# The first three tiles of a phase multiplied before the norm is known, in a two-layer decoder trunk

## Chip, cores and metric

One core of a Trainium2 chip runs the whole kernel in one launch. The metric is the time of an execution on the device in microseconds (us). Time before: 1978.98 us, the median of 3 runs (1977.27 to 1979.56).

## What is computed

256 tokens of width 1024 pass two layers. Each has a mixer (layer 0: mLSTM and block attention; layer 1: differential attention) and a product-key expert network, PEER, with 8 heads, 128 keys per half and 128x128 experts. Ahead of each stands an RMSNorm with scale and shift that depend on a conditioning vector. Cut to what matters here:

```python
def rms_norm(x, g):
    y = xf * lax.rsqrt(jnp.mean(xf * xf, axis=-1, keepdims=True) + EPS)
    return y * g

h = rms_norm(x, norm_mix_g[layer]) * (1.0 + sc1) + sh1
x = x + g1 * mixer(h)                 # layer 0: mlstm_moba_mixer, layer 1: diff_attention_mixer
h = rms_norm(x, norm_ffn_g[layer]) * (1.0 + sc2) + sh2
x = x + g2 * peer_ffn(h, ...)

# peer_ffn: qry = h @ wq (16 slices of 128), sub = qry . keys,
# top 16 of 128 per half, top 16 of the 256 sums, then
# sum over the experts chosen of gate * gelu(u_e . h) * v_e
```

## The kernel before

**Layout and tiles.** Activations lie transposed, features on the partitions: `xT` is 8 blocks (`kd`) of 128 features by 256 tokens. A column tile of a weight matrix is 1024x128, one DMA of 512 KB on SP's queue into a ring of `raw` buffers (`load`, L146). Float32 products are made of three: ACT casts the weight to its high part `hi` (L159), DVE subtracts to get the low part `lo` (L162), both into rings of three in `stream`; the activation has `hhi` and `hlo` likewise. `mm_col` issues for every kd hi by hhi (L185), hi by hlo (L186), lo by hhi (L187): 24 matmuls of 128x256 a tile. The first three tiles of a phase run together, each two kd behind the one before it (`SKEW`), 72 matmuls, so that they can follow `h` as it is made; the tiles after them run one by one (`col_tiles`, L191).

**The program.** Four phases follow each other: mixer0 (to 184 us of the span), peer0 (to 1003), mixer1 (to 1157), peer1 (to the end). A phase starts where the phase before writes the last block of the residual `xT` (L414 after a mixer, L952 after the peer). Each block is squared on ACT (L279), added up on DVE (L281, but for the last block), and the sum over the features is taken by matmuls with a column of ones (L290). `keep_warm` (L268) puts 3 and 5 matmuls of zeros around these (`WARM`). Then DVE makes the mean (`nv`, L299, L301), POOL the power -1/2 (`nr`, L262), PE spreads it over the partitions (L306, result `rb`), and `norm_apply` makes per kd: `ht` = x times channel weight `gsc` times `rb` on DVE (L315), `hhi` = ht + shift on ACT (L318), `hlo` on DVE (L328). `first_tiles` (L208) and the list `late` place the splits of the first three weight tiles between these steps.

**A peer** (`peer_body`, L819) takes 16 tiles of `wq`: tile i gives a query copy `qry` on ACT (L849), a score matmul pair per tile (`scores`, L976), a copy `sub` (L979) and the top-16 search on DVE (L985 to L989: MAX, MAX_INDEX, MATCH_REPLACE, MAX, MAX_INDEX per half and head). A credit (`credit`, from -3.0, more for every tile) decides how many of these stand on DVE behind the `lo` of each tile. After the 16 tiles, 128 tiles of `u` follow (`h_tile`), their search work still spread in between, and then the products with `v` (L921 to L923).

**Mixer1** (`mixer1`, L707) takes 16 q and k tiles and two blocks of values (L237 to L239). Each q tile with its k tile makes a head (`diff_head`): squares (L360), their sums by matmul (L363), DVE (`qv`, L365), POOL's power (`qr`, L262), PE (L372), two copies to `qrows` (L374, L375) and PE again (L382). Between, DVE multiplies the modulation weights of the later phases (`ada`, L252), whose raw tiles come through the same ring. All engines run their instructions in order.

## Time and profile before

| what | value |
| --- | --- |
| median of 3 runs | 1978.98 us |
| profiled execution, its own time | 1980.2 us |
| its span | 1978.4 us |
| PE busy | 1932.3 us, 98% |
| DVE, ACT busy | 1481.9 us, 75%; 1123.5 us, 57% |
| POOL busy | 47.1 us, 2% |
| chain that ended last | 87% PE, 6% issue, 3% DVE |

The span is the stretch from the first to the last instruction that the profiler saw; the execution's time is a little longer. The chain follows, from the last instruction back, what each one waited for.

### The profile page before, as it was taken

Reading aid. Unit: us, or ns where it says so; the run is one execution under the profiler, and the core shown is the slowest. Engines: PE = TensorE matmul, PEld = TensorE weight load, DVE = VectorE, ACT = ScalarE, POOL = GpSimd, SP = SyncE. Lnnn points to the kernel's source line nnn. Section 1 sums busy time; section 2 is a strip of 40 time slices with the busy share of each in tenths; the row PEclk is TensorE's granted clock in tenths of the full one; section 3 lists DMA queues with packets and bytes.
Section 4 is the critical chain, followed back from the end, with each engine's and each line's share of the span. In section 5 each row is a group of like instructions: output and inputs, shape, how many; then the busy total and the mean of one; then the engine's idle time right before and its main releaser. Section 6 shows DMA issues by size and latency. Waiting matters only on the chain.

```text
span 1978.4 us, 34700 instructions
## 1 busy us (share of the span) xinstructions
PE 1932.3 (98%) x13229; PEld 1754.7 (89%) x13229; DVE 1481.9 (75%) x3064; ACT 1123.5 (57%) x2137; POOL 47.1 (2%) x37
## 2 busy tenths in 40 slices
PE   5999999999999999999999999999999999999999
PEld 4888999999999788888878799999999988888887
DVE  8987999678887566777568789987788865556655
ACT  4655555777775444444456555557777744444443
POOL 0020000000000000000012100000000000000000
PEclk7999999999999999999999999999999999999999
DMA  8863355445445677898347233554545455559660
GB/s 333 289 207 133 108 174 190 162 165 164 161 160 171 194 220 217 327 349 299 129 168 235 75 136 118 184 181 153 171 151 170 160 163 195 196 193 359 226 201 22
DMA packets 103990, 376.43 MB, mean 190 GB/s; under 512 B 11536, under 2 KB 12944, under 8 KB 103696
## 3 DMA queue, kind: packets, MB, share of 16 engines
q1 hardware_dynamic: 103824, 374.22, 56.0%
q8 instruction: 104, 1.70, 0.3%
q14 instruction: 62, 0.51, 0.1%
HBM read 373.12 MB, written 1.05 MB: 189 GB/s over the span
## 4 chain that ended last, share of the span: by engine, by line
PE 87%; issue 6%; DVE 3%; DMA 2%; ACT 1%; POOL 1%; POOLq 0%; ACTq 0%; DVEq 0%
PE ps_h L185 15%; PE ps_h L187 14%; PE ps_h L186 14%; PE ps_acc L921 11%; PE ps_acc L923 11%; PE ps_acc L922 11%; PE ps_g L1108 3%; DMA raw<-in_ada_w_dram 1%; PE ps_l L389 1%; DVE raw L252 1%; PE ps_acc L976 1%; DVE lo L162 1%; PE ps_h L237 1%; PE ps_h L239 1%; PE ps_h L238 1%
## 5 line engine op out<-in xcount | busy, mean ns | idle before, releaser
L159 ACT CAST hi<-raw 128x1024 fp32r<-128x1024 f32 x613 | 644.8, 1053 | 714.4 <-PE ps_acc L922 313.4
L162 DVE TENSOR_TENSOR lo<-raw,hi 128x1024 fp32r<-128x1024 f32 x613 | 748.2, 1221 | 347.0 <-ACT hi L159 344.6
L185 PE MATMUL ps_h<-h,hi 128*128 128x256 f32 x2504 | 725.6, 290 | 8.0 <-ACT h L449 3.4
L187 PE MATMUL ps_h<-h,lo 128*128 128x256 f32 x2504 | 712.3, 285 | 0.4 <-DVE lo L162 0.4
L186 PE MATMUL ps_h<-h,hi 128*128 128x256 f32 x2504 | 711.5, 284 | 0.4 <-DVE h L451 0.4
L185 PEld LDWEIGHTS ps_h<-h,hi 128*128 128x128 f32 x2504 | 481.9, 193 | 13.9 <-ACT h L449 4.2
L187 PEld LDWEIGHTS ps_h<-h,lo 128*128 128x128 f32 x2504 | 481.9, 192 | 2.8 <-DVE lo L162 1.1
L186 PEld LDWEIGHTS ps_h<-h,hi 128*128 128x128 f32 x2504 | 482.5, 193 | 1.9 <-DVE h L451 0.7
L921 PE MATMUL ps_acc<-hi,act 128*128 128x512 f32 x1024 | 399.2, 391 | 5.6 <-ACT act L902 5.6
L922 PE MATMUL ps_acc<-hi,act 128*128 128x512 f32 x1024 | 400.0, 391 | 0.0
L923 PE MATMUL ps_acc<-lo,act 128*128 128x512 f32 x1024 | 399.8, 391 | 0.0
L921 PEld LDWEIGHTS ps_acc<-hi,act 128*128 128x128 f32 x1024 | 192.6, 188 | 45.6 <-ACT act L902 6.0
L922 PEld LDWEIGHTS ps_acc<-hi,act 128*128 128x128 f32 x1024 | 193.2, 189 | 41.1 <-DVE act L903 0.7
L923 PEld LDWEIGHTS ps_acc<-lo,act 128*128 128x128 f32 x1024 | 192.8, 188 | 40.4 <-DVE lo L162 0.7
L252 DVE CUSTOM_DVE_ANT_0 raw<-raw,crow,small 128x1024 f32<-128x1024 f32 x96 | 122.7, 1279 | 23.0 <-DMA raw<-in_ada_w_dram 22.9
L1085 ACT ACTIVATE oi<-iota,it 128x128 f16<-128x128 f16 x320 | 108.0, 406 | 0.0
L1095 DVE TENSOR_TENSOR og<-oj,gt 128x1024 f16<-128x1024 f16 x128 | 87.8, 686 | 12.4 <-PE ps_g L1108 12.2
L1116 DVE TENSOR_TENSOR A<-A,ps_g 128x256 f32<-128x256 f32 (+25 forms) x214 | 69.2, 346 | 31.0 <-PE ps_g L1108 30.3
L969 ACT ACTIVATE A<-ps_h 128x256 f32<-128x256 f32 (+20 forms) x240 | 76.9, 321 | 3.9 <-PE ps_h L187 3.9
L903 DVE TENSOR_TENSOR act<-A,act 128x1024 fp32r<-128x1024 f32 x64 | 77.8, 1218 | 0.0
L1108 PE MATMUL ps_g<-oi,og 128*128 128x128 f16 x1024 | 73.3, 222 | 0.0
L902 ACT CAST act<-A 128x1024 fp32r<-128x1024 f32 x64 | 72.2, 1131 | 0.0
(305 smaller groups left out, 1671.6 us busy)
## 6 DMA issues: line engine op xcount, KB each, us to landing
raw<-in_uT_dram SPq DMA_DIRECT2D x256, 512.0 KB, 3.5
raw<-in_v_dram SPq DMA_DIRECT2D x256, 512.0 KB, 4.4
raw<-in_ada_w_dram SPq DMA_DIRECT2D x96, 512.0 KB, 5.2
raw<-in_wq_dram SPq DMA_DIRECT2D x32, 512.0 KB, 4.5
raw<-in_ev_in_dram SPq DMA_DIRECT2D x21, 512.0 KB, 5.0
raw<-in_od_in_dram SPq DMA_DIRECT2D x16, 512.0 KB, 4.6
raw<-in_ev_v_dram SPq DMA_DIRECT2D x8, 512.0 KB, 4.0
raw<-in_ev_out_dram SPq DMA_DIRECT2D x8, 512.0 KB, 4.4
```

What stands on the lines that cost most here:

```text
L159: nc.scalar.copy(hi, raw)
L162: self.last_lo = nc.vector.tensor_tensor(out=lo, in0=raw, in1=hi.bitcast(F32), op=ALU.subtract)
L185: nc.tensor.matmul(ps, lhsT=whi[:, s], rhs=ahi[:, kd, :], start=kd == kds[0], stop=False)
L186: nc.tensor.matmul(ps, lhsT=whi[:, s], rhs=alo[:, kd, :], start=False, stop=False)
L187: nc.tensor.matmul(ps, lhsT=wlo[:, s], rhs=ahi[:, kd, :], start=False, stop=kd == kds[-1])
L252: nc.vector.tensor_tensor_reduce(w, w, self.crow, 1.0, self.small[:, ab:ab + 1], ALU.mult, ALU.add, m)
L921: nc.tensor.matmul(acc[q], lhsT=xhi, rhs=vhi[:, c], start=m == 0, stop=False)
L922: nc.tensor.matmul(acc[q], lhsT=xlo, rhs=vhi[:, c], start=False, stop=False)
L923: nc.tensor.matmul(acc[q], lhsT=xhi, rhs=vlo[:, c], start=False, stop=m == NEXP - 1)
L1085: nc.scalar.activation(oi[:, k, :], self.iota, AF.Square, scale=-1.0, bias=tabs["i"][:, t0 + k:t0 + k + 1])
L1095: nc.vector.tensor_tensor(out=og, in0=oj.unsqueeze(1).to_broadcast(og.shape), in1=tabs["g"][:, :, ts].unsqueeze(2).to_broadcast(og.shape), ...
L1108: nc.tensor.matmul(pv[:, k, :], lhsT=og[:, w, :, k], rhs=oi[:, k, :], start=w == 0, stop=w == 1)
```

## The change

At the start of peer0, mixer1 and peer1 the first three tiles are no longer made from `h`. `raw_start` forms `pre` = x times `gsc`, not normalised, as a high part (8 ACTIVATE, L220) and a low part (8 on DVE, L221), with two more columns that hold the shift (L216, L217), and multiplies the three tiles with these: 72 matmuls of 128x258. Their weight splits lie in buffers of their own (`first`) and not in the ring of three. `raw_finish` turns the sums into outputs `fz`: the shift's column is copied (L230), the sum is multiplied by the norm factor on DVE (L231) and the shift's product added on ACT (L232). `norm_rstd` and `norm_apply` come behind, for the tiles 3 and on, of which three run together now in mixer1 and in the peers (`phase_tiles`). `WARM` is (0, 0): the 24 matmuls of zeros go, and the last square is added on DVE, so that one pair of sums (L308) is left of two. `first_tiles` and `late` go. The pools move: a peer's `wq` ring (5 buffers) lies in a pool of its own that closes before `A0` opens, and mixer1's ring has 9 buffers in place of 10. In mixer0 two pool names move, its instructions don't. The diff, cut to its core:

```diff
@@ -38,11 +38,9 @@
 V0_AT = 5
 SIDE_P2 = 52
 SKEW = 2
-LATE1 = ("stat", (None, 2), (None, 4))
-LATEP = (None, None, (None, 3))
 ROWS0 = {4: 1, 5: 1, 6: 1, 7: 1, 8: 4}
 AHEAD = 2
-WARM = (3, 5)
+WARM = (0, 0)
 SIDE_AT = 14
 LATE_RING = 15
...
@@ -207,21 +194,52 @@
             self.ready.append(self.wsplit(self.feed.pop(0)))
         return self.ready.pop(0)
 
...
+    @staticmethod
+    def next_raw(pool, bufs):
+        return pool.tile([P, 1024], F32, tag="raw", name="raw", bufs=bufs)
+
+    def raw_start(self, pool, layer, which, aps, tags, homes=()):
+
+
+        nc = self.nc
+        self.outs = [pool.tile([P, T], F32, tag="fz", name="fz", bufs=3) for _ in tags]
+        self.rstd = pool.tile([P, T], F32, name="rstd")
+        pre = pool.tile([P, 2, KD, T + 2], F32R, name="pre")
         ring, self.raw_ring = self.raw_ring, self.stream_ring
+        raws = [self.load(a) for a in aps[:len(tags)]]
         self.raw_ring = ring
+        pairs = list(homes)
+        pairs += [pool.tile([P, 2, 1024], F32R, tag=f"f{i}", name="first") for i in range(len(pairs), len(tags))]
+        ws = [self.split(raw, (p[:, 0], p[:, 1])) for raw, p in zip(raws, pairs)]
+        sh0 = 0 if which == 0 else 24
+        sh = self.mod[:, layer, sh0:sh0 + KD].unsqueeze(2).to_broadcast([P, KD, 2])
+        nc.scalar.copy(pre[:, 0, :, T:], sh)
+        nc.vector.tensor_tensor(out=pre[:, 1, :, T:], in0=sh, in1=pre[:, 0, :, T:].bitcast(F32), op=ALU.subtract)
+        for kd in range(KD):
+            x, g = self.xT[:, kd, :], self.gsc[:, layer, which, kd:kd + 1]
+            nc.scalar.activation(pre[:, 0, kd, :T], x, AF.Copy, scale=g)
+            nc.vector.scalar_tensor_tensor(pre[:, 1, kd, :T], x, g, pre[:, 0, kd, :T].bitcast(F32), op0=ALU.mult,
+                                           op1=ALU.subtract)
+        pss = [self.psum(t) for t in tags]
+        self.mm_col([ps[:, :T + 2] for ps in pss], ws, (pre[:, 0], pre[:, 1]))
+        return pss
+
+    def raw_finish(self, pool, ps, rstd, z):
+
+        b = pool.tile([P, 1], F32, tag="fb", name="fb", bufs=3)
+        self.nc.scalar.copy(b, ps[:, T:T + 1])
+        self.nc.vector.tensor_mul(z, ps[:, :T], rstd)
+        self.nc.scalar.activation(z, z, AF.Identity, bias=b)
+        return z
+
+    def phase_tiles(self, pool, aps, first, rb, act, tags, rest=None):
+
+        self.nc.scalar.copy(self.rstd, rb)
+        done = [self.raw_finish(pool, ps, self.rstd, z) for ps, z in zip(first, self.outs)]
+        n = len(first)
+        yield from enumerate(done)
+        for i, ps in self.col_tiles(aps[n:], act, tags, ws=[self.take(a) for a in aps[n:n + len(tags)]], rest=rest):
+            yield n + i, ps
 
     def mm_row(self, pss, aps, act):
 
...
@@ -707,22 +720,25 @@
     def mixer1(self):
         nc, tc, hp = self.nc, self.tc, self.hp
         w_in = self.io["od_in"]
-        ws = self.first_tiles([w_in[0], w_in[8], w_in[1]], LATE1)
         with ExitStack() as st:
             pool = st.enter_context(tc.tile_pool(name="mix1", bufs=1, reuse_waits="tile"))
             self.psum_phase(st, "psm1")
-            self.raw_ring = (pool, 10)
+            cols = [w_in[8 * k + hd] for hd in range(NH) for k in range(2)]
+            self.raw_ring = (pool, 9)
+            homes = [pool.tile([P, 2, 1024], F32R, tag=t, name="first") for t in ("yhi", "ylo")]
+            ht = pool.tile([P, KD, T], F32, tag="v", name="ht")
+            bias = self.alibi(pool)
+            first = self.raw_start(pool, 1, 0, cols, ("l", "l", "t"), homes)
             h = hp.tile([P, 2, KD, T], F32R, tag="x", name="h")
             hhi, hlo = h[:, 0], h[:, 1]
-            self.norm_apply(1, 0, self.norm_rstd(), pool.tile([P, KD, T], F32, tag="ylo", name="ht"), hhi, hlo)
+            rb = self.norm_rstd()
+            self.norm_apply(1, 0, rb, ht, hhi, hlo)
             h = (hhi, hlo)
-            with tc.issue_after(self.last_h.ins), tc.issue_after(self.last_t.ins):
-                self.qk_setup(pool, Cols.od_qn, Cols.od_kn)
-                og = pool.tile([P, 1], F32, name="og")
-                nc.vector.tensor_scalar_mul(og, self.small[:, Cols.onorm:Cols.onorm + 1], 1.0 - LAM_INIT)
-                bias = self.alibi(pool)
-            v = pool.tile([P, TT, 1024], F32, name="v")
-            yhi = pool.tile([P, KD, T], F32R, name="yhi")
+            self.qk_setup(pool, Cols.od_qn, Cols.od_kn)
+            og = pool.tile([P, 1], F32, name="og")
+            nc.vector.tensor_scalar_mul(og, self.small[:, Cols.onorm:Cols.onorm + 1], 1.0 - LAM_INIT)
+            v = pool.tile([P, TT, 1024], F32, tag="v", name="v")
+            yhi = pool.tile([P, KD, T], F32R, tag="yhi", name="yhi")
             ylo = pool.tile([P, KD, T], F32R, tag="ylo", name="ylo")
             lam = pool.tile([P, 1], F32, name="lam")
             live, zs, vhave = [], [], [0]
@@ -734,10 +750,9 @@
                     yield
                 vhave[0] = 4 * n + 4
 
-            cols = [w_in[8 * k + hd] for hd in range(NH) for k in range(2)]
             od_v = [[self.io["od_v"][n, w4] for w4 in range(4)] for n in range(2)]
             self.feed = cols[3:V0_AT + 1] + od_v[0] + cols[V0_AT + 1:V1_AT + 1] + od_v[1] + cols[V1_AT + 1:]
-            for i, ps in self.col_tiles(cols, h, ("h", "h", "l"), ws=ws):
+            for i, ps in self.phase_tiles(pool, cols, first, rb, h, ("t", "h", "h")):
                 z = pool.tile([P, T], F32, tag="z", name="z", bufs=8)
                 self.last_z = nc.scalar.copy(z, ps)
                 zs.append(z)
@@ -818,33 +833,35 @@
 
     def peer_body(self, layer, side, st):
         nc, tc = self.nc, self.tc
-        ws = self.first_tiles([self.io["wq"][layer, i] for i in range(3)], LATEP)
         self.psum_phase(st, f"psp{layer}")
         tab = st.enter_context(tc.tile_pool(name=f"tab{layer}", bufs=1, reuse_waits="tile"))
         oh = st.enter_context(tc.tile_pool(name=f"oh{layer}", bufs=2, reuse_waits="tile"))
         hp = self.hp
-        a0 = st.enter_context(tc.tile_pool(name=f"a0{layer}", bufs=1, reuse_waits="tile"))
+        wqp = tc.tile_pool(name=f"wqp{layer}", bufs=1, reuse_waits="tile")
+        wp = wqp.__enter__()
         tabs = {"i": tab.tile([P, T], F32, name="it"), "j": tab.tile([P, T], F16, name="jt"),
                 "g": tab.tile([P, 2, T], F16, name="gt")}
-        A0 = a0.tile([P, 32, T, 2], F32, name="A0")
-
-        scr = tc.tile_pool(name=f"scr{layer}", bufs=1, reuse_waits="tile")
+        scr = tc.tile_pool(name=f"scr{layer}", bufs=1, reuse_waits="tile", side="right")
         sp = scr.__enter__()
         h2 = hp.tile([P, 2, KD, T], F32R, tag="x", name="h2")
         hhi, hlo = h2[:, 0], h2[:, 1]
         ht = sp.tile([P, KD, T], F32, tag="eq", name="ht", bufs=1)
-        self.norm_apply(layer, 1, self.norm_rstd(), ht, hhi, hlo)
+        self.raw_ring = (wp, 5)
+        self.next_raw(*self.raw_ring)
+        wq = [self.io["wq"][layer, i] for i in range(16)]
+        first = self.raw_start(wp, layer, 1, wq, ("acc",) * 3)
+        rb = self.norm_rstd()
+        self.norm_apply(layer, 1, rb, ht, hhi, hlo)
         h = (hhi, hlo)
 
         keys = sp.tile([P, 2, P], F32, name="keys")
         nc.sync.dma_start(keys, self.io["keysT"][layer])
         vals = sp.tile([P, TT, 16, TOPK], F32, name="vals")
         idxs = sp.tile([P, TT, 16, TOPK], U32, name="idxs")
-        self.raw_ring = (sp, 5)
         subs = []
         topk = chain(self.stage1(sp, subs, vals, idxs), self.top_k(sp, vals, idxs, tabs))
         credit, live = -3.0, True
-        for i, ps in self.col_tiles([self.io["wq"][layer, i] for i in range(16)], h, ("acc",) * 3, ws=ws):
+        for i, ps in self.phase_tiles(wp, wq, first, rb, h, ("acc", "h", "h")):
             q = sp.tile([P, T], F32, tag="qry", name="qry", bufs=2)
             nc.scalar.copy(q, ps)
             if i:
@@ -858,8 +875,10 @@
                     credit -= next(topk)
 
         self.raw_ring = self.stream_ring
+        wqp.__exit__(None, None, None)
+        a0 = st.enter_context(tc.tile_pool(name=f"a0{layer}", bufs=1, reuse_waits="tile"))
         u, v = self.io["uT"][layer], self.io["v"][layer]
-        A, i = [A0], 0
+        A, i = [a0.tile([P, 32, T, 2], F32, name="A0")], 0
         while live:
             self.h_tile(u[i], h, A, i)
             if i == 0:
```

Where the instructions stand now. **ACT at the start of peer0.** `sq` are the squares, `first` the weight casts of the first three tiles, `hi` those of the tiles after. Before:

```order
L279 ACTIVATE sq<-xT 128x256
L159 CAST hi<-raw 128x1024
L279 ACTIVATE sq<-xT 128x256 x2
L159 CAST hi<-raw 128x1024
L318 ACTIVATE h_2066<-ht,mod 128x256 x8
```

And with the change:

```order
L297 ACTIVATE sq<-xT 128x256 x3
L154 CAST first<-raw 128x1024
L297 ACTIVATE sq<-xT 128x256
L154 CAST first<-raw 128x1024 x2
L216 CAST pre<-mod 128x8x2
L220 ACTIVATE pre<-xT,gsc 128x256 x8
L154 CAST hi<-raw 128x1024 x3
L230 COPY fb<-ps_acc 128x1 x3
L336 ACTIVATE h_2037<-ht,mod 128x256 x8
L237 COPY rstd<-ps_g 128x256
L154 CAST hi<-raw 128x1024
L232 ACTIVATE fz<-fz,fb 128x256 x3
```

All eight `pre` stand behind the square of the last block (the single L297) and behind two weight casts; the three `fz` stand behind the cast of tile 6.

**DVE in peer0 around the weight tiles 6 to 8** (`lo` the low part of a weight tile, MAX, MAX_INDEX and MATCH_REPLACE the search). Before, the `lo` of tiles 7 and 8 and what stands between them:

```order
L162 TENSOR_TENSOR lo<-raw,hi 128x1024
L988 MAX vals<-mr 128x8
L985 MAX vals<-sub 128x8
L989 MAX_INDEX idxs<-vals,mr 128x8
L986 MAX_INDEX idxs<-vals,sub 128x8
L987 MATCH_REPLACE mr<-vals,sub 128x128
L162 TENSOR_TENSOR lo<-raw,hi 128x1024
```

And with the change, where the search begins:

```order
L231 TENSOR_TENSOR fz<-ps_acc,rstd 128x256 x3
L155 TENSOR_TENSOR lo<-raw,hi 128x1024 x2
L1004 MAX vals<-sub 128x8 x2
L1005 MAX_INDEX idxs<-vals,sub 128x8
L1006 MATCH_REPLACE mr<-vals,sub 128x128
L1005 MAX_INDEX idxs<-vals,sub 128x8
```

The two `lo` are those of tiles 6 and 7. From the first MAX 43 search instructions follow in a row, and then the `lo` of tile 8. Before, the same 43 stood 18, 10, 10 and 5 ahead of the `lo` of the tiles 5, 6, 7 and 8. From that `lo` on both orders are the same.

**PE in mixer1 behind the second three tiles** (L363 is L377 now, L372 is L386, L382 is L396, L753 is L768, L237 is L255). Before:

```order
L186 MATMUL ps_h<-h,hi 128x256
L363 MATMUL ps_g<-ind_83,qsq 128x2 x2
L753 MATMUL ps_g<-lam_pr,ones 128x2
L187 MATMUL ps_h<-h,lo 128x256
L185 MATMUL ps_h<-h,hi 128x256
L363 MATMUL ps_g<-ind_83,qsq 128x2 x2
```

And with the change:

```order
L174 MATMUL ps_h<-h,lo 128x256
L377 MATMUL ps_g<-ind_83,qsq 128x2 x2
L768 MATMUL ps_g<-lam_pr,ones 128x2
L377 MATMUL ps_g<-ind_83,qsq 128x2 x2
L386 MATMUL ps_g<-ident,qr 4x128 x2
L377 MATMUL ps_g<-ind_83,qsq 128x2 x2
L396 MATMUL ps_g<-qrows,qsel 128x256 x2
L377 MATMUL ps_g<-ind_83,qsq 128x2 x2
L255 MATMUL ps_h<-hi,h 128x512
```

The head's small products stood among the matmuls of the tiles 3 to 5; now those tiles are done before them, and nothing of a tile stands between.

## Rows read from the trace of the kernel before

**Rows 1.** The page, part 1: busy time, share, instructions of each engine.

```profile
PE 1932.3 (98%) x13229; PEld 1754.7 (89%) x13229; DVE 1481.9 (75%) x3064; ACT 1123.5 (57%) x2137; POOL 47.1 (2%) x37
```

**Rows 2.** Windows: busy by engine; before the DMA share stands PE's granted clock.

```profile
184.00:189.00 5.00, 3.83 (x24) 2.40 (x22) 1.82 (x7) 1.77 (x4) 0.70 (x1) 1.00 0.80 238
204.00:224.00 20.00, 20.00 (x170) 19.88 (x169) 20.00 (x92) 9.55 (x18) 0.00 (x0) 1.00 0.43 145
224.00:274.00 50.00, 50.00 (x419) 49.75 (x418) 49.24 (x205) 23.60 (x39) 0.00 (x0) 1.00 0.35 117
1007.60:1014.00 6.40, 5.17 (x22) 4.88 (x23) 5.02 (x11) 2.32 (x5) 0.06 (x1) 0.50 0.01 3
```

**Rows 3.** Timeline, start of peer0: start, duration, engine, instruction, count, [idle before].

```profile
184.13 0.28 PE L187 MATMUL ps_h<-yhi,lo 128*128 128x256 f32 x1
184.44 0.48 DVE L414 SCALAR_TENSOR_TENSOR xT<-ps_h,mod,xT 128x256 f32<-128x256 f32 x1 [0.36 <-PE ps_h L187]
185.02 0.42 ACT L279 ACTIVATE sq<-xT 128x256 f32<-128x256 f32 x1 [2.21 <-DVE xT L414]
185.34 1.03 ACT L159 CAST hi<-raw 128x1024 fp32r<-128x1024 f32 x1
...
187.32 0.71 PE L306 MATMUL ps_g<-ident,nr 128*128 128x128 f32 x4
...
189.14 0.61 PE L185 MATMUL ps_acc<-h,hi 128*128 128x256 f32 x3 [1.11 <-ACT h L318]
...
189.78 0.39 PE L186 MATMUL ps_acc<-h,hi 128*128 128x256 f32 x1
```

**Rows 4.** Timeline of DVE, peer0: the last `hlo`, the search, the weight `lo`.

```profile
195.38 0.48 DVE L328 SCALAR_TENSOR_TENSOR h<-ht,mod,h 128x256 fp32r<-128x256 f32 x1 [0.19 <-ACT h L318]
...
200.31 0.48 DVE L985 MAX8 vals<-sub 128x8 f32<-128x128 f32 x2
...
211.48 1.21 DVE L162 TENSOR_TENSOR lo<-raw,hi 128x1024 fp32r<-128x1024 f32 x1
212.61 0.28 DVE L988 MAX8 vals<-mr 128x8 f32<-128x128 f32 x1
...
213.78 1.21 DVE L162 TENSOR_TENSOR lo<-raw,hi 128x1024 fp32r<-128x1024 f32 x1
...
220.73 1.20 DVE L162 TENSOR_TENSOR lo<-raw,hi 128x1024 fp32r<-128x1024 f32 x1
```

**Rows 5.** Timeline of PE, peer0: score matmuls, each ahead of a tile.

```profile
198.20 1.06 PE L976 MATMUL ps_acc<-keys,qry 128*128 128x128 f32 x8
199.01 0.36 PE L185 MATMUL ps_h<-h,hi 128*128 128x256 f32 x1
...
208.61 0.61 PE L976 MATMUL ps_acc<-keys,qry 128*128 128x128 f32 x4
...
222.11 0.61 PE L976 MATMUL ps_acc<-keys,qry 128*128 128x128 f32 x4
```

**Rows 6.** Timeline, mixer1: last block of x, first three tiles, what follows them.

```profile
1003.12 0.48 DVE L952 SCALAR_TENSOR_TENSOR xT<-ps_h,mod,xT 128x256 f32<-128x256 f32 x1
...
1010.86 0.41 PE L186 MATMUL ps_h<-h,hi 128*128 128x256 f32 x1
...
1021.06 1.28 DVE L252 CUSTOM_DVE_ANT_0 raw<-raw,crow,small 128x1024 f32<-128x1024 f32 x1
...
1023.08 2.61 POOL L262 TENSOR_TENSOR qr<-qv,mhalf 128x8 f32<-128x8 f32 x1 [4.38 <-DVE gsc L255]
...
1025.75 0.38 PE L372 MATMUL ps_g<-ident,qr 128*4 128x128 f32 x2 [0.46 <-POOL qr L262]
...
1026.56 0.41 DVE L375 TENSOR_TENSOR qrows<-ps_g,qrows 4x256 fp32r<-4x256 f32 x1
...
1033.97 0.48 PE L237 MATMUL ps_h<-hi,h 128*128 128x512 f32 x1
```

**Rows 7.** The page, part 6: count, KB each, median us from issue to landing.

```profile
raw<-in_ada_w_dram SPq DMA_DIRECT2D x96, 512.0 KB, 5.2
```

More of the change, by code (lines that the diff above doesn't have):

```diff
@@ L89, in setup @@
         self.raw_ring = self.stream_ring = (self.stream, 3)
-        self.feed, self.ready, self.late = [], [], []
+        self.feed, self.ready = [], []
         self.tmp = ctx.enter_context(tc.tile_pool(name="tmp", bufs=2, reuse_waits="tile"))
@@ L150, in load, with split @@
         return raw
-    def split(self, raw, late=None):
+    def split(self, raw, parts=None):
         nc = self.nc
-        hi = self.stream.tile([P, 1024], F32R, tag="hi", name="hi")
-        lo = self.stream.tile([P, 1024], F32R, tag="lo", name="lo")
-        def high():
-            nc.scalar.copy(hi, raw)
-        def low():
-            self.last_lo = nc.vector.tensor_tensor(out=lo, in0=raw, in1=hi.bitcast(F32), op=ALU.subtract)
-        for part, kd in zip((high, low), late or (None, None)):
-            if kd is None:
-                part()
-            else:
-                self.late.append((kd, part))
+        hi, lo = parts or [self.stream.tile([P, 1024], F32R, tag=t, name=t) for t in ("hi", "lo")]
+        nc.scalar.copy(hi, raw)
+        self.last_lo = nc.vector.tensor_tensor(out=lo, in0=raw, in1=hi.bitcast(F32), op=ALU.subtract)
         return hi, lo
@@ L208, in take @@
         return self.ready.pop(0)
-    def first_tiles(self, aps, late):
-        ring, self.raw_ring = self.raw_ring, self.stream_ring
-        ws = []
-        for a, when in zip(aps, late):
-            if when == "stat":
-                with self.tc.issue_after(self.last_sq.ins), self.tc.issue_after(self.last_add.ins):
-                    ws.append(self.split(self.load(a)))
-            elif when and when[0] is None:
-                with self.tc.issue_after(self.last_sq.ins):
-                    ws.append(self.split(self.load(a), when))
-            else:
-                ws.append(self.split(self.load(a), when))
-        self.raw_ring = ring
-        return ws
+    @staticmethod
@@ L314, in norm_apply @@
         for kd in kds:
-            self.last_t = nc.vector.scalar_tensor_tensor(t[:, kd, :], self.xT[:, kd, :], self.gsc[:, layer, which, kd:kd + 1], r,
-                                                         op0=ALU.mult, op1=ALU.mult)
+            nc.vector.scalar_tensor_tensor(t[:, kd, :], self.xT[:, kd, :], self.gsc[:, layer, which, kd:kd + 1], r,
+                                           op0=ALU.mult, op1=ALU.mult)
             sh = self.mod[:, layer, sh0 + kd:sh0 + kd + 1]
-            self.last_h = nc.scalar.activation(hhi[:, kd, :], t[:, kd, :], AF.Identity, bias=sh)
+            nc.scalar.activation(hhi[:, kd, :], t[:, kd, :], AF.Identity, bias=sh)
             if kd > kds[0]:
                 self.norm_lo(layer, sh0, t, hhi, hlo, kd - 1)
-            self.late.sort(key=lambda e: e[0])
-            while self.late and self.late[0][0] <= kd:
-                with self.tc.issue_after(self.last_h.ins), self.tc.issue_after(self.last_t.ins):
-                    self.late.pop(0)[1]()
         self.norm_lo(layer, sh0, t, hhi, hlo, kds[-1])
@@ L436, in mixer0 @@
             r = self.norm_rstd()
-            xn = pool.tile([P, KD, T], F32, tag="yhi", name="xn")
+            xn = pool.tile([P, KD, T], F32, tag="qk", name="xn")
             for half in range(2):
@@ L499, in mixer0 @@
                     bias = self.alibi(pool)
+                    yhi, ylo = [pool.tile([P, KD, T], F32R, name=n) for n in ("yhi", "ylo")]
                     self.qk_setup(pool, Cols.ev_qn, Cols.ev_kn)
@@ L875, in peer_body @@
         scr.__exit__(None, None, None)
-        a1p = tc.tile_pool(name=f"a1{layer}", bufs=1, reuse_waits="tile")
+        a1p = tc.tile_pool(name=f"a1{layer}", bufs=1, reuse_waits="tile", side="right")
         A.append(a1p.__enter__().tile([P, 32, T, 2], F32, name="A1"))
@@ L896, in peer_body @@
                     a1p.__exit__(None, None, None)
-                    late = st.enter_context(tc.tile_pool(name=f"late{layer}", bufs=1, reuse_waits="tile"))
+                    late = st.enter_context(tc.tile_pool(name=f"late{layer}", bufs=1, reuse_waits="tile", side="right"))
                     self.raw_ring = (late, LATE_RING)
```

4 lines of the change are left out of this document (1 added, 3 removed).

## Prediction

> **What bounds the kernel now.** I read the page's busy shares first, then the windows, then the timeline of each place that the change touches. PE is busy for 1932.3 of 1978.4 us [rows 1]: only 46 us of the span are not matmul, so a change at the phase starts can gain no more than the holes that stand there, and each new hole on PE is lost time, since nothing later has room to make it up. The windows show where the next engine stands behind PE [rows 2]: in peer0 from 204 to 224 us DVE is busy for 20.00 of 20.00 us, and from 224 to 274 for 49.24 of 50.00. PE is full there too. In this stretch of a peer, then, two engines are both at their limit, and whatever comes late on DVE stays late. Below 0.2% (4 us) a measurement of this kernel can't tell a change from none.
>
> **The hole that the change goes for.** The last matmul of mixer0 starts at 184.13 and PE could go on at 184.25; the first product of peer0 starts at 189.14, the first that needs h's low part at 189.78, and from there 72 products run at one per 0.12 us until 198.20 [rows 3, 5]. So 5.3 us of PE hold only sums, zeros and one small broadcast. The same picture stands ahead of peer1. In mixer1 the last x is written at 1003.12 and the steady products begin at 1010.86 [rows 6].
>
> **Peer: the first three tiles.** What they wait for now is `pre`, and by the order all of it stands on ACT behind the last square and two weight casts. From rows 3: the last square 185.02, casts at 185.34 and 186.29 (a cast holds ACT for about 0.95), the first high part about 187.9. On DVE the subtractions of these casts and the last addition to the sum come first; the third one can't start before the second of these casts has ended, about 187.4, and takes 1.2, the shift's columns 0.2, the first low part 0.5: 189.4. So the dense products begin at 189.4 in place of 189.78, take 8.42 as before plus 72 x 2 columns (0.07), and end at 197.9: **0.3 gained**. The two ends: nothing gained, if one more step on ACT or DVE comes late, and 1.5, if the products of high parts alone keep PE going from 187.9.
>
> **Peer: the second three tiles.** The broadcast (now L324) is behind the 72 products on PE. The norm chain that used to be hidden in the hole hence starts at 197.9. From L306 to the first product of h it took 189.14 - 187.32 = 1.82 [rows 3], a new hole of that size. From L306 to the end of the last `hlo` it took 195.86 - 187.32 = 8.54 with one weight subtraction (1.13 to the next start, rows 4) among it, so 7.4 now: 205.3. By the order two tiles run in this stretch, 48 products, paced by h: their end is the last `hlo` plus six products and a little, 206.3. Then PE wants the scores of tiles 0 and 1, whose queries come from `fz`. On ACT the cast of tile 6 stands ahead of the three `fz`, and it waits for tile 4's last use of its buffer, 206.0; cast to 206.95, three `fz` at about 0.36 and one query copy (a 128x256 step frees ACT after 0.32, rows 3): scores at 208.5. So PE has a second hole of 2.2 us. Tile 3 follows these two pairs of scores by 0.81 [rows 5], 0.4 a pair, and takes 2.88 (24 x 0.12), 209.3 to 212.2; three more pairs precede tile 6: 213.4. Before, tile 6 began behind its pair at 208.61 + 0.4 = 209.0. **PE is 4.4 late here**, whatever DVE does.
>
> **Peer: the search on DVE.** The scores came at 198.20 and the search began at 200.31 [rows 4, 5]. Now the subtraction of tile 7 stands ahead of the first MAX; its cast follows the query copies on ACT (208.8 to 209.85), so it ends at 211.0. The 43 search steps that stood among four weight subtractions now stand in a row: from 200.31 to 213.78 is 13.47, less three subtractions of 1.13 gives 10.1. The subtraction of tile 8 starts at 211.0 + 10.1 = 221.1, in place of 213.78: DVE is 7.3 late. From there on the order is the same as before and DVE has no slack: 0.76 us in 50. PE's lag grows until it meets this: tile 10 had its `lo` at 220.73 + 1.20 = 221.93 [rows 4] and needed it at its third product, 222.11 + 0.4 + 0.24 = 222.75 [rows 5], 0.8 of lead. 7.3 - 0.8 = **6.5 us a peer, 13.0 for both**. Ends: 4.4 (DVE makes it up) and 7.3 (no lead). I take 6.5, since rows 2 and 4 are of this very stretch.
>
> **Mixer1.** The last x is at 1003.12; the same chain as in the peer (184.44 to 189.4, 5.0) with two more DVE steps of mixer1 among it gives some 1009.0, in place of 1010.86. The products take 8.42 and, as slow at first as now (the clock, below), 1.6 more: end 1019.0. The second three tiles, three at once, end 10.9 later: 1.82 to the first product, 8.64 of products (72 x 0.12), 0.4 of waiting for h: 1029.9. Then the head's first small products stand on PE one behind the other with nothing between. ACT: cast 1028.05, three `fz`, two z, one bias, square: about 1031.6. DVE's `qv` has two L252 ahead of it; the raw tile of the second is requested when an earlier L252 has freed its buffer, about 1027.4; 5.2 to land [rows 7] and 1.28 [rows 6] make 1033.9. POOL's power 0.2 later takes 2.61: PE's L386 at 1036.8. From L372 to the end of `qrows` it took 1.2 [rows 6]: L396 at 1038.1, a pair of sums, and the values start at 1038.9, in place of 1033.97. The same tiles lie before this point in both orders, so **mixer1 loses 4.9**. Ends: 2.5 (no wait for that raw tile, 1.2 less, and as much again made up later in the phase) and 6.
>
> **What costs nothing.** The buffers: the first wq tiles are loaded long before; mixer1's ring of 9 holds the tiles 3 to 5, four of the values and two more. The 24 products of zeros stood in the hole. The second pair of sums, the same. The weight tiles 3 and on, whose loads move on SP's queue, are used behind the 72 products, 8 us and more after the start, and a tile of 512 KB took 5.2 to land [rows 7]. The cover of all these is the hole itself.
>
> **The sum.** 6.5 + 6.5 + 4.9 = 17.9 us. The profiled execution took 1980.2, so 1998.1; against the median of 1978.98 it is **1996.9**.
>
> **The clock.** PE's granted clock was 0.50, the lower level of 1.2 GHz, from 1007.6 to 1014 [rows 2], after PE had had only sums, zeros and the wait for POOL. The products ran from 1010.86 to 1014 at that level: half of these 3.1 us, **1.6**, is what the fall cost. At the start of peer0, with its products of zeros, the clock was 1.00 [rows 2]. They go, and in 184.25 to 189.4, in 197.9 to 199.7 and in 206.3 to 208.5 PE has almost nothing. Since no row shows a peer without them, I leave 0 to 1.6 a fall out of the sum and in the range. The Trainium skill, page "TensorE: Matmul & The Clock Gate", section "Why this matters for your kernels", says that idle gaps between bursts of matmuls bring the clock down to its lower level; by it each of the peers would fall at its start, the second rival below. The trace agrees in mixer1; for the peers nothing here shows it yet.
>
> **The rivals.**
> - *The search catches up.* Only the holes on PE are lost, 4.4 + 4.4 + 4.9 = 13.7, so 1992.7. For it: DVE is 75% busy over the span [rows 1]. Against it: the windows, and that PE waits for the same `lo`. Decides at slack of over 2 us on DVE before 274; there is 0.8. Chance 0.15.
> - *The clock falls in both peers.* 17.9 + 3.2 (one fall each): 2000.1; with a second fall each 2003.3. Chance 0.22.
> - *Faster.* The raw products fill the hole: if the high and low parts of the first blocks are made while the residual's last tiles run, PE starts at about 185.5, ends at 194, and has the norm factor by then; each peer gains about 4, mixer1 about 4: 1967. It decides where the first `pre` starts: it must be before the last x (184.44), and the order has it behind. Chance 0.08.
> - *Nothing.* The gain of 0.3 to 1.8 a phase outweighs what is lost, since ACT's waits are shorter than I made them and DVE's search lies where PE is late anyway: within 4 us of 1979. Chance 0.07.
>
> **How the numbers follow.** Forecast 0.48, the rivals as given. The range 1985 to 2004 takes in the forecast with its ends (4.4 to 7.3 a peer, 2.5 to 6 in mixer1: 1990 to 2000), the catching up and the clock; it leaves out the two last. Faster by over 0.2%: 0.08; within 0.2%: 0.07; slower by over 0.2%: 0.85.
>
> **What the profile after would show.** Right: in peer0 first product about 189, broadcast 197.9, holes of 1.8 and 2.2 behind it, the `lo` of tile 8 about 7 us later against the last x than before, the values of mixer1 5 later. Wrong: a first raw product before 187, or scores of tile 0 before 207, or a `lo` of tile 8 before 216.

## The result and the profile after

The changed kernel takes **2013.43 us** (median of 4 runs, 2006.82 to 2016.0) against 1978.88 (4 runs, 1977.27 to 1979.56): 1.0171 times as long, 95% interval 1.0146 to 1.0196, so some 34.5 us slower. The forecast was 1996.9 with a range of 1985 to 2004. The direction was right, the size was half of it. Of two later kernels, early2c and best2, one execution each was far slower than the others (2707.66 and 6631.01 us): it is left out of their medians here, and since it was the profiled one, no phase is read from their traces.

The page, part 1, of the changed kernel (to hold beside [rows 1]):

```profile
PE 1946.7 (97%) x13193; PEld 1766.5 (88%) x13193; DVE 1494.4 (74%) x3100; ACT 1138.7 (57%) x2185; POOL 60.8 (3%) x37
```

PE is busy 14 us longer with 36 instructions fewer: part of the loss is not waiting but the same products run slower. To see where, I read in each trace the last write of x of a phase (L414, now L428, before the peers; L952, now L971, before mixer1) and took the time from one to the next (for peer1, to the end of the span). The profiled execution is one run, so these are single numbers:

| kernel (profiled execution) | peer0 | mixer1 | peer1 |
| --- | --- | --- | --- |
| before | 818.7 | 153.8 | 821.5 |
| changed: longer by | 9.1 | 18.2 | 7.9 |
| forecast: longer by | 6.5 | 4.9 | 6.5 |

The windows of the changed kernel, columns as in [rows 2] (PE, PEld, DVE, ACT, POOL busy, then PE's granted clock):

```profile
190.00:196.00 6.00, 6.00 (x28) 6.00 (x29) 6.00 (x11) 4.14 (x7) 3.15 (x1) 0.52 0.18 48
1030.00:1046.00 16.00, 11.38 (x89) 10.67 (x88) 13.80 (x32) 10.90 (x24) 1.38 (x1) 0.99 0.60 224
1046.00:1076.00 30.00, 27.63 (x78) 17.73 (x78) 11.99 (x44) 9.21 (x25) 4.51 (x3) 0.55 0.29 101
1076.00:1160.00 84.00, 83.77 (x521) 66.76 (x520) 64.65 (x214) 51.32 (x148) 15.40 (x10) 1.00 0.46 146
1045.70:1073.00 27.30, 24.63 (x66) 15.71 (x67) 10.77 (x37) 9.00 (x24) 4.81 (x3) 0.50 0.33 114
212.80:216.30 3.50, 3.50 (x19) 3.50 (x18) 3.50 (x18) 0.66 (x3) 0.00 (x0) 0.51 0.67 235
```

And the kernel before, where its value products begin:

```profile
1034.00:1060.00 26.00, 26.00 (x124) 18.02 (x123) 19.40 (x70) 13.92 (x33) 2.55 (x1) 1.00 0.71 244
```

At the start of peer0, and for 27 us in mixer1 (1045.7 to 1073.0), PE ran at its lower level of 1.2 GHz; before, this part of mixer1 ran at 1.00. A short second fall lies in peer0 from 212.8 to 216.3. In the 30 us from 1046 on PE was granted 0.55 of its clock while busy for 27.63: about 0.45 x 27.63 = 12 us of work lost, more than the whole loss that I had forecast for the phase.

The timeline of peer0 in the changed kernel, DVE and PE (answers to [rows 3 to 5]):

```profile
185.13 0.48 DVE L428 SCALAR_TENSOR_TENSOR xT<-ps_h,mod,xT 128x256 f32<-128x256 f32 x1 [1.39 <-PE ps_h L174]
...
213.79 0.48 DVE L1004 MAX8 vals<-sub 128x8 f32<-128x128 f32 x2
...
224.32 1.22 DVE L155 TENSOR_TENSOR lo<-raw,hi 128x1024 fp32r<-128x1024 f32 x1
```

```profile
188.57 0.72 PE L172 MATMUL ps_acc<-pre,first 128*128 128x258 f32 x3 [0.83 <-ACT pre L220]
...
189.98 0.58 PE L173 MATMUL ps_acc<-pre,first 128*128 128x258 f32 x1 [0.69 <-DVE pre L221]
...
200.95 0.60 PE L324 MATMUL ps_g<-ident,nr 128*128 128x128 f32 x4
...
202.66 0.51 PE L172 MATMUL ps_h<-h,hi 128*128 128x256 f32 x2 [1.11 <-ACT h L336]
...
211.42 0.82 PE L995 MATMUL ps_acc<-keys,qry 128*128 128x128 f32 x5 [2.32 <-ACT qry L866]
...
218.22 1.26 PE L995 MATMUL ps_acc<-keys,qry 128*128 128x128 f32 x8 [0.85 <-ACT qry L866]
219.23 0.36 PE L172 MATMUL ps_h<-h,hi 128*128 128x256 f32 x1
```

The last x is 0.69 later than before, so 0.7 is to be taken off each. The first low part then comes at 189.3 (forecast 189.4), the hole behind the broadcast is 1.71 (1.82), the wait of the scores 2.32 (2.2). The raw stream alone is off: it ends at 200.3 and not 197.9, since its first 6 us ran at 0.52. The low part of tile 8, 213.78 before [rows 4], starts at 223.6, 2.5 later than forecast, nearly all of it this clock.

But PE itself is later than I had it. Tile 6 (the last row) starts at 219.23 - 0.69 = 218.5, forecast 213.4; before, it was 208.97 [rows 5: 208.61 and its pair of scores]. So PE is 9.6 late here and not 4.4: 2.4 more from the raw stream, about 1.7 from the second fall under tile 3 (half of 3.4), and 0.85 from a third wait, for the queries, that I had not forecast. And among PE's waits in peer0 up to 290 us there is none for a `lo` (in peer1 one, of 0.3). DVE's row of 43 steps did come late, as forecast, but PE was as late without it.

The timeline of mixer1 in the changed kernel, PE:

```profile
1030.18 0.61 PE L324 MATMUL ps_g<-ident,nr 128*128 128x128 f32 x4
...
1031.90 0.39 PE L172 MATMUL ps_t<-h,hi 128*128 128x256 f32 x1 [1.11 <-ACT h L336]
...
1042.88 0.61 PE L377 MATMUL ps_g<-ind,qsq 128*128 128x2 f32 x4 [1.82 <-ACT qsq L374]
...
1047.29 0.59 PE L386 MATMUL ps_g<-ident,qr 128*4 128x128 f32 x2 [2.96 <-POOL qr L280]
1048.95 1.01 PE L377 MATMUL ps_g<-ind,qsq 128*128 128x2 f32 x4 [1.07 <-ACT qsq L374]
1049.89 0.80 PE L396 MATMUL ps_g<-qrows,qsel 4*128 4x256 f32 x2
1051.49 0.77 PE L255 MATMUL ps_h<-hi,h 128*128 128x512 f32 x1
```

Before, the values began 30.9 behind the last x [rows 6]; now it is 1051.49 - 1012.88 = 38.6, so 7.8 more (forecast 4.9). The other 10.4 of the 18.2 are lost behind this point, where PE waits for nothing: from 1051.5 to 1073.0 it is busy for all 21.5 us at 0.50, and half of that is 10.8.

### The profile page after: what moved, and what is told of

The parts are those of the page before. It is cut to its first block, busy times and chain, and to the rows that moved or that the text cites. A ratio compares the mean times of both kernels' runs of the same rounds, so it can differ in the third digit from the quotient of the medians.

```text
span 2014.2 us, 34740 instructions
## 1 busy us (share of the span) xinstructions
PE 1946.7 (97%) x13193; PEld 1766.5 (88%) x13193; DVE 1494.4 (74%) x3100; ACT 1138.7 (57%) x2185; POOL 60.8 (3%) x37
## 4 chain that ended last, share of the span: by engine, by line
PE 88%; DVE 6%; DMA 2%; ACT 1%; issue 1%; POOL 1%; ACTq 0%; DVEq 0%; POOLq 0%
PE ps_h L172 14%; PE ps_h L173 14%; PE ps_h L174 14%; PE ps_acc L941 12%; PE ps_acc L942 12%; PE ps_acc L940 12%; PE ps_g L1127 3%; DVE lo L155 1%; PE ps_l L403 1%; DMA raw<-in_ada_w_dram 1%; DVE raw L270 1%; PE ps_h L255 1%; PE ps_h L256 1%; ACT hi L154 1%; PE ps_g L396 1%
## 5 line engine op out<-in xcount | busy, mean ns | idle before, releaser
L154 ACT CAST hi<-raw 128x1024 fp32r<-128x1024 f32 x604 | 634.9, 1053 | 703.3 <-PE ps_acc L941 320.2
L155 DVE TENSOR_TENSOR lo<-raw,hi 128x1024 fp32r<-128x1024 f32 x604 | 737.0, 1221 | 342.2 <-ACT hi L154 341.3
L172 PE MATMUL ps_h<-h,hi 128*128 128x256 f32 x2464 | 712.4, 290 | 8.9 <-ACT h L463 3.0
L174 PE MATMUL ps_h<-h,lo 128*128 128x256 f32 x2464 | 700.1, 284 | 0.7 <-DVE lo L155 0.7
L173 PE MATMUL ps_h<-h,hi 128*128 128x256 f32 x2464 | 700.0, 284 | 0.6 <-DVE h L465 0.4
L172 PEld LDWEIGHTS ps_h<-h,hi 128*128 128x128 f32 x2464 | 473.7, 192 | 14.7 <-ACT h L463 3.8
L173 PEld LDWEIGHTS ps_h<-h,hi 128*128 128x128 f32 x2464 | 474.5, 193 | 2.4 <-DVE h L342 0.7
L174 PEld LDWEIGHTS ps_h<-h,lo 128*128 128x128 f32 x2464 | 473.9, 192 | 2.8 <-DVE lo L155 1.6
L1135 DVE TENSOR_TENSOR A<-A,ps_g 128x256 f32<-128x256 f32 (+25 forms) x214 | 69.2, 345 | 30.9 <-PE ps_g L1127 30.3
```

What stands on the lines that cost most here:

```text
L154: nc.scalar.copy(hi, raw)
L155: self.last_lo = nc.vector.tensor_tensor(out=lo, in0=raw, in1=hi.bitcast(F32), op=ALU.subtract)
L172: nc.tensor.matmul(ps, lhsT=whi[:, s], rhs=ahi[:, kd, :], start=kd == kds[0], stop=False)
L173: nc.tensor.matmul(ps, lhsT=whi[:, s], rhs=alo[:, kd, :], start=False, stop=False)
L174: nc.tensor.matmul(ps, lhsT=wlo[:, s], rhs=ahi[:, kd, :], start=False, stop=kd == kds[-1])
```

## The experiments

Two theories. **The place**: the norm chain, the search and the head's small products stand where PE must wait for them, and in such empty stretches the clock falls; move them and the loss goes. **The extra work**: `pre`, `fz`, the columns, the buffers cost this much by themselves. At the side of the first stands the question how much is the clock and how much the waits. Diffs are against the changed kernel unless said otherwise; "longer" is against before, from the profiled execution; the median of before in these comparisons was 1977.45 to 1979.98.

**One phase alone.** mixer_only takes `peer_body` and its start from the kernel before, peers_only takes `mixer1` from there.

> The changed start in mixer1 alone, both peers as before. By the trace of the change mixer1 took 18.2 us longer than before (from the last x of peer0 to the last x of mixer1: 171.99 against 153.80). If the loss is made inside mixer1, this kernel takes 1979 + 18 = 1997 us (1993 to 2000). If mixer1 is slow only because of what the new peer0 leaves behind (later loads, another pool), it takes under 1986.

> The changed start in both peers alone, mixer1 as before. By the trace of the change peer0 took 9.1 and peer1 7.9 us longer. If the phases add up: 1979 + 17 = 1996 us (1992 to 1999). If the loss of the peers depends on mixer1's: under 1988.

Measured: 1997.78 us (ratio 1.0095, interval 1.0079 to 1.0112) and 1992.6 (1.0071, 1.0054 to 1.0088). Peer0 and peer1 are 6.6 and 7.1 longer in the second, mixer1 0.0; in the first mixer1 is 10.3 longer, the peers -0.2 and 0.4. The phases add up roughly (18.5 + 13.3 against 34.5), so each makes its loss itself. In mixer_only's profiled run the lower clock behind the second three tiles lasted 10 us (1037.1 to 1047.3) and not 27 (windows of that kernel):

```profile
1038.00:1047.00 9.00, 6.91 (x22) 4.90 (x22) 2.27 (x7) 4.25 (x11) 2.60 (x2) 0.50 0.41 144
1047.00:1077.00 30.00, 30.00 (x160) 21.71 (x159) 24.06 (x84) 16.15 (x43) 1.64 (x1) 0.99 0.45 147
```

The same instructions of mixer1 in the same order, 17.1 us less at the lower level, and mixer1 is 7.9 shorter: the length of such a fall differs from run to run, which fits the wide spread of the changed kernel (9 us, before 2). A second pair says the same: start_zeros and search_late, below, share their mixer1 too, had 27.3 and 10.2 us at 0.50 there, and took 17.7 and 10.0 longer than before. From these pairs I estimate 0.45 us lost for each us at the lower level; the fall of the changed kernel then cost some 12, and without it mixer1 would be about 6 longer (forecast 4.9).

For the peers the two numbers of the table say less than they seem to. In peers_only both peers fell at the start and again behind the wait for the scores (186.1 to 192.9 and 210.0 to 213.4 in peer0), as peer0 of the changed kernel did, and yet they are only 6.6 and 7.1 longer, not 9.1 and 7.9. So a single phase of this length is good to some 2 us.

**Zeros in the empty places.**

```diff
+                if i == 0:
+                    self.keep_warm(6, "l")
...
+                if i == 1:
+                    with tc.issue_after(self.last_sum.ins):
+                        self.keep_warm(14, "l")
```

(m1_zeros_pin; the first value product is also held behind the head's last small product.) And start_zeros:

```diff
-WARM = (0, 0)
+WARM = (8, 8)
```

> The changed kernel with 20 matmuls of zeros in mixer1: 6 before the first head's sums and 14 in the wait for POOL's power, the order of the rest held. Theory of the clock: the half clock from 1046 to 1076 follows from PE's empty stretch; with the zeros it stays at 1.00, which gives back about half of those 29 us less what the zeros themselves cost: 10 to 13 us, 2001 to 2004. Theory of the waits (the time goes into the waits for POOL, ACT and DVE, the clock costs little): no change, 2011 to 2015.

> The changed kernel with 8 matmuls of zeros before and 8 behind the sums of squares at each of the three starts (and two pairs of sums again). Theory of the clock: the half clock at the start of the raw products (5.8 us in peer0, so 2.6 to 2.9 lost, the like in peer1, 8 us in mixer1) goes: 5 to 8 us less, 2005 to 2009. Theory of the waits: 2011 to 2015, or longer, since the zeros behind the sums delay the first raw products.

Measured: 2005.93 (1.0135, 1.0118 to 1.0152) and 2009.22 (1.0141, 1.012 to 1.0163). The first lies between the theories, nearer to that of the clock: mixer1 is 9.8 longer and not 18.2, since behind a remaining wait of 1.4 for POOL the clock still fell for 7 us. The total of the second decides little, as its four runs spread from 2002.35 to 2010.55; its windows say more. At the peers' start the clock stayed up, but behind the wait for the scores it fell in both peers, here in peer0:

```profile
189.00:195.00 6.00, 5.88 (x49) 5.88 (x50) 6.00 (x12) 3.82 (x7) 3.01 (x1) 1.00 0.16 42
208.00:211.50 3.50, 3.50 (x16) 3.50 (x17) 2.28 (x9) 2.24 (x5) 0.00 (x0) 0.51 0.48 151
```

49 products in 6 us in place of 28, and peers 6.3 and 7.0 longer in place of 9.1 and 7.9. A steadier mark is the last scores of a peer, those of tile 15, some 61 us behind the last x before: they come 7.5 later than that in both peers here, and 8.6 to 9.4 later in the eight peers of the four kernels without zeros there (the changed kernel, peers_only, m1_zeros_pin, heads_later). So the fall at a peer's start costs 1.1 to 1.9 more than the zeros do. Mixer1 stayed at 17.7, its costly fall lies elsewhere.

**The norm factor early** (early_norm, excerpt; `after` makes the broadcast and `norm_apply`):

```diff
+            if hook and step == HOOK:
+                hook()
...
+        self.norm_pow()
...
+        self.mm_col([ps[:, :T + 2] for ps in pss], ws, (pre[:, 0], pre[:, 1]), hook=after)
```

> The changed kernel with the norm factor made early: its mean and power ahead of the low parts of pre, its broadcast and norm_apply inside the stream of raw products and not behind it. Theory of the place (the loss comes from the norm chain standing behind the 72 raw products, so that it opens holes on PE, which also let the clock fall in mixer1): h is ready when the raw products end, both holes in the peers and those in mixer1 close: peers at most 2 us over before each, mixer1 at most 4, 1980 to 1988 us. Theory of the extra work (pre, fz, the buffers and the pools cost by themselves): peers still 5 or more over before, 2000 to 2012.

Measured: 1996.81 (1.0088, 1.0071 to 1.0105), between the two. Mixer1 fell from 18.2 to 4.8, but the peers stayed 7.8 and 7.0 longer. Its timeline shows two new waits in peer0: the broadcast, put behind three raw products, waited 1.4 for POOL, and the scores, now ahead of the second three tiles, 3.1 for `fz`. early_all, the same with zeros and a later search, took 1996.63: neither touches these waits.

> The early norm, 14 zeros at each start, and the search credit at -9. Theory of the place: at or under the early norm alone by what the clock at the three starts costs, 1.5 to 3 us a phase: 1974 to 1982 us; at best 4 us faster than before, since the hole of 5.3 us shrinks by the 0.3 to 1 us that the raw products begin earlier. Theory of the extra work: 1995 to 2008.

**The search later** (search_late, against start_zeros):

```diff
-        credit, live = -3.0, True
+        credit, live = -9.0, True
```

> The kernel with zeros at the starts (2009.2 us), and the peers' search credit starting at -9 and not -3, so that 12 search steps and not 43 stand ahead of the low part of tile 8. Theory of the prediction (the row of 43 steps makes DVE late by 2 us more than PE's two holes): each peer 1.5 to 2.5 us shorter, peer0 from 825.0 to about 823, 2005 us. Theory of the holes alone (DVE's lag is made up later): both peers within 0.5 us of what they were, 2009.

Measured: 2002.98 (1.0135, 1.0111 to 1.0159); peer0 6.6 longer (6.3 without), peer1 5.2 (7.0). The total decides nothing, since mixer1 with the same instructions had the shorter fall and is 7.7 shorter; and one peer speaks for either theory. The last scores of peer0 do decide (PE of before, start_zeros, search_late):

```profile
245.35 0.61 PE L976 MATMUL ps_acc<-keys,qry 128*128 128x128 f32 x4
```

```profile
252.05 0.61 PE L995 MATMUL ps_acc<-keys,qry 128*128 128x128 f32 x4
```

```profile
254.17 0.61 PE L995 MATMUL ps_acc<-keys,qry 128*128 128x128 f32 x4
```

Behind the last x of mixer0 (184.44, 183.63, 185.72) that is 60.9, 68.4 and 68.5, and peer1 gives the same 7.5: PE is as late with the row of 43 steps as without it. In this kernel the row costs nothing that can be seen; the holes on PE make the loss. early2 and early2c asked again, with the two new waits of early_norm gone: the broadcast held behind the fifth step, and

```diff
+        ahead = next(more)
         self.nc.scalar.copy(self.rstd, rb)
```

so that the second three tiles stand ahead of `fz` and the scores.

> The early norm again, with the two waits taken away that it had put in place of the old ones: the broadcast is held behind the fifth step of the raw products (it had stood behind three of them and waited for POOL 1.4), and the scores of the first tiles stand behind the second three tiles (they had waited for fz 3.1). 8 and 6 zeros at each start. Theory of the place: PE has no hole over 0.5 us from the first raw product to tile 6; what is left is DVE, where 52 search steps (12 us) stand in a row ahead of tile 9's low part: 2 to 5 us a peer, mixer1 at most 3: 1983 to 1992. Theory of the extra work: 5 or more a peer as before, 1994 to 1998.

> The same, with the search credit starting at -12, so that at most 9 search steps stand between two low parts. Theory of the place with DVE's row as the rest: both peers within 1 us of before, mixer1 at most 3 over: 1976 to 1983. If the row of search steps does not count: as the kernel beside it. Theory of the extra work: 1994 to 1998.

Measured: 1999.78 (1.0104, 1.0085 to 1.0122) and 1991.42 (1.0074, 1.0051 to 1.0096); -12 in place of -3 is worth 6 to 8 (by ratios and by medians), though the four runs of early2c spread over 10 us and nothing shows in which phase it gained. In early2 peer0 is 3.6 and peer1 5.5 longer, and the row behind the 52 search steps shows part of it (PE of that kernel):

```profile
223.79 0.39 PE L177 MATMUL ps_h<-h,lo 128*128 128x256 f32 x1 [1.92 <-DVE lo L156]
```

So the search in a row does cost, once the holes ahead of it no longer make PE late as well. Mixer1 went up to 14.4 in early2, since its head's products again stood bare behind the second three tiles, with a wait of 5.0 for POOL among them. That is why early2's total missed; early2c has the same order in mixer1 and missed as well.

**The splits in between** (best1, and best2 with mixer1 as before):

```diff
+            if kd in (1, 3):
+                p = pairs[len(ws)]
+                ws.append(self.split(raws[len(ws)], (p[:, 0], p[:, 1])))
```

> The early norm with the scores behind the second three tiles in the peers (in mixer1 the head's chain comes as early as in the first early norm), the search credit at -12, four zeros at each start, and the splits of the second and third weight tile placed behind the second and fourth step of pre, on ACT and DVE, and no longer ahead of the first. By the order the first raw products wait for one square, the shift's columns, one step of pre on ACT and one on DVE: some 2 us behind the last x in place of 5. Theory of the place: the raw products begin about 3 us earlier in each phase; peers 1 to 3 us under before, mixer1 from 2 under to 4 over: 1972 to 1981 us. Theory of the extra work: 1988 or more.

> The same peers, with mixer1 as it was before the change. Theory of the place: mixer1 as before, each peer 1 to 3 us under before: 1973 to 1977 us, faster than both. Theory of the extra work: 1986 or more.

Measured: 1991.84 (1.0065, 1.0049 to 1.0082) and 1978.71 (0.9997, 0.9987 to 1.0006). In best1 the peers are -0.5 and 0.7 longer, with all the extra work still in them: their loss was the place. How much each of the moves gave is not separated, and the kernel before was not run with the later search. The gain of 1 to 3 a peer did not come. Mixer1 is 12.5 longer, with an empty stretch and 24 us at the lower clock behind it (windows of best1):

```profile
1029.00:1033.00 4.00, 1.28 (x6) 0.98 (x6) 2.92 (x7) 2.82 (x9) 1.59 (x1) 0.85 0.85 305
1033.00:1055.00 22.00, 21.94 (x59) 14.13 (x60) 8.35 (x31) 5.52 (x13) 4.25 (x2) 0.50 0.37 131
```

**Mixer1's empty stretch closed with work** (heads_later: the changed kernel with this edit alone, in `mixer1`; best3: best1 with it):

```diff
-                self.advance(live)
+                if i > 5:
+                    self.advance(live)
```

> The changed kernel; in mixer1 the work of the first heads begins only when the value products are issued, so that these (and not an empty wait) stand behind the second three tiles and cover POOL's power. Nothing else is changed. Theory of the empty stretch (the wait, 6 to 8 us, and the half clock behind it make mixer1's loss, but for the hole at the broadcast and the slow start): mixer1 2 to 5 us over before and not 18, the clock at 1.00 from the second three tiles on: 1997 to 2002 us. Theory of the start (the raw products and the rest of the new mixer1 cost it): mixer1 still 9 or more over, 2004 or more.

> The kernel with every cause removed in the peers (1991.8 us, peers within 1 us of before, mixer1 12.5 over) and the heads of mixer1 behind the value products. Theory of the empty stretch: mixer1 from 3 under to 3 over before, in all 1975 to 1982 us, about as before. A gain of 2 us or more over before would show that the early raw products pay once nothing waits behind them. Theory of the start: 1988 or more.

heads_later: 2000.11 (1.0111, 1.0094 to 1.0128), as its first theory had it; mixer1 4.8 longer in place of 18.2, the peers 8.0 and 7.3. The stretch that held the fall (window of heads_later):

```profile
1041.00:1071.00 30.00, 29.89 (x179) 24.35 (x177) 21.14 (x61) 15.73 (x38) 5.83 (x3) 1.00 0.69 224
```

179 products in 30 us where the changed kernel had 78 (a different mix, as the heads' work now stands later). Three lines of the program give back 13.3 of the 34.5 us. The edit takes away both the waits ahead of the values and the fall, so its 13.4 in mixer1 is not the clock's alone; what the 4.8 that stay are made of is not shown. One wait of 2.14 is left ahead of the first value product (at 1040.1), and behind this one the clock stayed at 1.00. best3 missed: 1996.78 (1.0091, 1.0074 to 1.0108), mixer1 14.5 longer. The values started 25.9 behind the last x, 5 earlier than before, but one wait was left behind them (PE of best3, then its windows):

```profile
1043.13 0.38 PE L409 MATMUL ps_g<-ident,qr 128*4 128x128 f32 x2 [2.16 <-POOL qr L292]
```

```profile
1040.00:1044.00 4.00, 1.84 (x10) 1.01 (x10) 1.32 (x3) 1.53 (x3) 2.55 (x1) 1.00 0.90 315
1044.00:1070.00 26.00, 26.00 (x91) 20.42 (x92) 11.90 (x44) 7.27 (x22) 0.00 (x0) 0.51 0.33 111
```

**What is left to gain** (best5: best2 with the split of tile 3 ahead of `norm_apply`; best4_4: that in all three phases, and four steps between a head's sums and its transposes).

> The peers of the kernel at 1979.2 us (early norm, interleaved splits, late search, four zeros), mixer1 as before the change, and in the peers the split of tile 3 ahead of the norm's steps on DVE, so that PE no longer waits 1.6 us for its low part. Theory of the place: 1 to 1.6 us a peer under before, 1975 to 1977.5 us. If that wait only moves to the next one (the scores waiting for the queries 0.9 us, or the search): 1978 to 1980.

> The same with mixer1 changed too: early raw products, heads behind the value products, and the transposes of a head's norm factors four steps and not two behind its sums, so that POOL's 2.6 us lie behind tile work for the first heads. Theory of the empty stretch: without a wait of 2 us or more mixer1 keeps the clock at 1.00 and its values start 5 us earlier than before: mixer1 2 to 5 under before, 1971 to 1977 us in all. If any wait of about 2 us is left there, the clock falls again and mixer1 is 8 to 14 over: 1985 to 1992.

Measured: 1978.61 (0.9995, 0.9986 to 1.0004) and 2008.84 (1.0142, 1.012 to 1.0164). best5 is no version that beats before, as its second theory had it: the first low part of `pre` is used 2.4 behind the last x, where that of h had been used 5.3 behind it, and PE then waits again in what follows (its waits from 180 to 280 us; the one for `pre` is already in the 2.4):

```profile
PE ps_acc L1064 <- ACT qry L935: 0.9, 2, 0.7
PE ps_h L213 <- DVE lo L157: 0.5, 1, 0.5
PE ps_acc L212 <- DVE pre L261: 0.4, 1, 0.4
PE ps_acc L213 <- DVE first L157: 0.4, 1, 0.4
```

3.0 - 1.8 = 1.2, and the peers are 0.9 and 0.5 shorter. best4_4 is slower than either theory: mixer1 is 32 longer, with waits of 2.1 and 2.2 us and two places with waits of 1.1 to 1.6, and a fall of the clock behind each of the four (3, 37, 10 and 7 us). A version of mixer1 with the new start and no such wait was not found.

## Why the prediction was wrong

- **The step that failed is the clock**, "I leave 0 to 1.6 a fall out of the sum and in the range". For mixer1 the sum has one fall, at its start; what the fall behind the second three tiles does to the value products stands in it at nothing. I had listed the waits there (1.7 for ACT, then POOL) and did not ask what they do to the clock. Of the 18.2 that mixer1 lost, 10.4 lie behind the first value product, at 0.50 with PE busy throughout; the two pairs of runs with a shorter and a longer fall put the whole of it at some 12. That is more than the miss outside the range, 9.4. The edit that closed the empty stretch with work brought mixer1 to 4.8 by taking away the fall and most of the waits ahead of it, so that this lies near the 4.9 of the sum is chance.
- **In the peers the sum was near by luck.** I had 6.5, made by DVE's row of 43 steps, with PE's own holes at 4.4 below it. The places came as forecast (first low part, the holes of 1.8 and 2.2, the row, each within 0.5 us of what it follows, except where the clock was low), and DVE was late. But PE did not wait for it: tile 6 came 9.6 late in peer0 of the changed kernel, and in start_zeros and search_late PE was 7.5 late with the row and without. The holes were mis-sized: the falls, and a third wait of 0.85, were not in the 4.4. Some 1 us of it is made up later in the phase, and so peers with zeros lost 6.3 and 7.0.
- **The size of a fall was taken from one row.** In [rows 2] a fall lasted 6.4 us, 3.1 of them with dense products, and I took 1.6 as the most that any fall costs. In the runs falls lasted from 3.4 us (peer0 behind the scores) to 37 (best4_4). The advice of the Trainium skill, page "TensorE: Matmul & The Clock Gate", section "Why this matters for your kernels", to leave no long idle gaps between bursts of matmuls, speaks against just this change; I applied it to the starts of the peers and not to every hole that I had found. The trace agrees with it in mixer1 of the changed kernel and in best1, best3 and best4_4, but not everywhere: the wait of 2.14 in heads_later and one of 2.27 in best3 (at 1018.2) had the clock at 1.00 behind them, and behind the wait of 2.3 for the scores it fell in peer0 of the changed kernel for 3.4 us and in its peer1 not at all.
- **Mixer1's waits were right in kind, 2.9 short in size** (7.8 at the values in place of 4.9). Of these the small products of the head at half clock are 2 (L386 to the values 4.2, forecast 2.1); most of the rest lies in the slow raw products.
- **The rivals.** "The clock falls in both peers" came true in kind: each peer without zeros fell at its start, most a second time. "The search catches up" (1992.7) was right that only PE's holes are lost in the changed kernel, and wrong in their size; with the holes closed the row does cost, as PE's wait of 1.9 in early2 shows. "Faster" fell with the order: the first low part was used 4.9 behind the last x, as the rows said. Even with `pre` moved as far forward as best5 has it, the gain is under what a measurement can tell. "Nothing" fell with the 34.5.

## What to carry to other kernels

Price a new wait on TensorE twice: the wait itself, and what the clock takes from the work behind it. Where waits of 2 us and more come in a place with little other PE work, look at the windows' clock column for the next tens of us, and cover the wait with products that are due anyway before trying zeros. And a change that starts work earlier must also move what follows it; here the norm chain and the heads' small products each cost more than the early start could give, and the search did so once the other holes were closed. And when a time comes out as forecast, look whether the engine waited for what the forecast names: in the peers it did not.

## What the runs showed that I had not expected

- Behind waits of about 2 us the granted clock stayed at 0.50 for 24 to 37 us while the windows show PE busy for 90% and more of it (the changed kernel, best1, best3, best4_4), and for 10 us in another run of the same order. What holds it down that long, and what ends it, no run here tells.
- In the peers the falls at the start ended after about 7 us, those behind the scores after 3.4, under the dense products of 256 and 258 columns; the falls of 24 us and more all lie under mixer1's mix of value and small products. Whether the mix is the cause was not tried.
